# Gather, running sum and projection on one core: groups of four scheduled tiles against hand-ordered single tiles with smaller stores

The chip is one Trainium2, the kernel uses one of its cores, and the metric is the device time in microseconds (us) of one execution.

The names used below: PE is the engine of matmuls (TensorE), DVE the vector engine, ACT the scalar engine, POOL the GpSimd engine, which issues the gathers here, and SP issues loads and stores. The granted clock is the mean share of PE's full clock that the chip allowed.

## The reference, cut to what matters

```python
B, S, N, D = (16, 4096, 2048, 512)
gathered = x[b_idx, indices, :]          # x fp32 [B,S,D], indices int64 [B,N], sorted
cs = np.cumsum(gathered, axis=1)         # running sum along the N gathered rows
return np.matmul(cs, w)                  # w fp32 [D,D], result fp32 [B,N,D]
```

There are 16 x 2048 = 32,768 rows, or 256 tiles of 128 rows. 67 MB are read and 67 MB are written.

## The kernel before

A gather of one tile is an indirect DMA issued by POOL. It converts fp32 to fp16 on the way (the page of the kernel before has 68.42 MB read from HBM, and 33.57 MB moved by the gathers' queue). PE multiplies the tile by a triangular matrix, which gives the sums within the tile, transposed (`pa`). DVE adds the last column of the tile before and writes `csT`. PE multiplies `csT` by `w` (`pb`), ACT copies `pb` to `ob`, and SP stores `ob`. A group of R tiles is interleaved so that each partition holds R neighbouring output rows, which makes runs of R x 2 KB in the store.

```python
    R = 4; Q = P // R; AHEAD = 10                      # groups of four tiles; ten groups ahead
    gp  = tile_pool(name="gp", bufs=R * (AHEAD + 2))   # 48 gather buffers of 128 x 512 fp16
    csp = tile_pool(name="csp", bufs=4);  outp = tile_pool(name="outp", bufs=5)
    psA = tile_pool(name="psA", bufs=3, space=PSUM); psB = tile_pool(name="psB", bufs=5, space=PSUM)
    ... # indices: two loads of 128 rows, w: one load on ACT's queue
    for k in range(KI):                                # indices to one per partition
        nc.vector.tensor_copy(out=idxf[:, k, :], in_=idx64[:, k, :].bitcast(U32)[:, 0::2])
        nc.tensor.transpose(out=idx_ps[:], in_=idxf[:, k, :], identity=ident[:])
        nc.vector.tensor_copy(out=idxg[:, k, :], in_=idx_ps[:])
    ...
    for g in range(AHEAD):
        gather(g)                                      # four indirect DMAs
    for g in range(G + 1):
        if g + AHEAD < G:
            gather(g + AHEAD)
        for r in range(R):
            if g < G:
                cumsum_tile(g, r)                      # 4 matmuls pa, DVE add -> csT
            if g > 0:
                project_tile(g - 1, r)                 # 4 matmuls pb, ACT copy; r==3: store 1 MB
```

The order of instructions on each engine is chosen by a scheduler.

Of the kernel before, what the change touches and what calls it, by code (L numbers as in the profile page):

```python
# [1 line left out]

# [5 lines left out]

P = 128
FP32 = mybir.dt.float32  # L10
FP16 = mybir.dt.float16
U32 = mybir.dt.uint32
I64 = mybir.dt.int64


@with_exitstack
def kernel(
    ctx: ExitStack,
    tc: tile.TileContext,
    x: bass.AP,  # L20
    indices: bass.AP,
    w: bass.AP,
    out: bass.AP,
):
    nc = tc.nc

    B, S, D = x.shape
    N = indices.shape[1]
    R = 4
    Q = P // R  # L30
    DC = D // P
    NT = N // P
    T = B * NT
    G = T // R
    GB = NT // R
    AHEAD = 10
    assert D == 512 and N % (R * P) == 0 and T % P == 0

    x_flat = x.rearrange("b s d -> (b s) d")

    const = ctx.enter_context(tc.tile_pool(name="const", bufs=1))
    gp = ctx.enter_context(tc.tile_pool(name="gp", bufs=R * (AHEAD + 2)))
    csp = ctx.enter_context(tc.tile_pool(name="csp", bufs=4))
    outp = ctx.enter_context(tc.tile_pool(name="outp", bufs=5))
    psA = ctx.enter_context(tc.tile_pool(name="psA", bufs=3, space=bass.MemoryType.PSUM))
    psB = ctx.enter_context(tc.tile_pool(name="psB", bufs=5, space=bass.MemoryType.PSUM))


    KI = T // P
    idx_rows = indices.rearrange("b (t p) -> (b t) p", p=P)  # L50
    idx64 = const.tile([P, KI, P], I64)
    for k in range(KI):
        nc.sync.dma_start(out=idx64[:, k, :], in_=idx_rows[k * P : (k + 1) * P, :])  # L53
    w32 = const.tile([P, DC, D], FP32)
    nc.scalar.dma_start(out=w32[:], in_=w.rearrange("(c p) d -> p c d", p=P))

    ident = const.tile([P, P], FP32)
    make_identity(nc, ident[:])

    ut = const.tile([P, R, Q], FP16)  # L60
    nc.gpsimd.memset(ut[:], 1.0)  # L61
    nc.gpsimd.affine_select(  # L62
        out=ut[:],
        in_=ut[:],
        compare_op=mybir.AluOpType.is_ge,
        fill=0.0,
        base=0,
        pattern=[[1, R], [R, Q]],
        channel_multiplier=-1,
    )  # L70

    idxf = const.tile([P, KI, P], FP32)
    idxg = const.tile([P, KI, P], U32)
    for k in range(KI):
        nc.vector.tensor_copy(out=idxf[:, k, :], in_=idx64[:, k, :].bitcast(U32)[:, 0::2])  # L75
        idx_ps = psB.tile([P, P], FP32, name="idx_ps", tag="pb")
        nc.tensor.transpose(out=idx_ps[:], in_=idxf[:, k, :], identity=ident[:])  # L77
        nc.vector.tensor_copy(out=idxg[:, k, :], in_=idx_ps[:])  # L78

    w16 = const.tile([P, DC, D], FP16)  # L80
    nc.scalar.copy(out=w16[:], in_=w32[:])  # L81

    gs = {}
    cst = {}

    def gather(g):
        for r in range(R):
            t = g * R + r
            g16 = gp.tile([P, D], FP16, name="g16")
            nc.gpsimd.indirect_dma_start(  # L90
                out=g16[:],
                out_offset=None,
                in_=x_flat,
                in_offset=bass.IndirectOffsetOnAxis(ap=idxg[:, t // P, t % P : t % P + 1], axis=0),
                element_offset=(t // NT) * S * D,
            )
            gs[t] = g16

    def cumsum_tile(g, r):
        if r == 0:  # L100
            cst[g] = csp.tile([P, DC, R, P], FP16, name="csT")
        csT = cst[g]
        g16 = gs.pop(g * R + r)
        pa = psA.tile([P, DC, R, Q], FP32, name="pa")
        for c in range(DC):
            nc.tensor.matmul(  # L106
                out=pa[:, c],
                lhsT=g16[:, c * P : (c + 1) * P],
                rhs=ut[:],
                start=(c == 0),  # L110
                stop=(c == DC - 1),
            )
        dst = csT[:, :, :, r * Q : (r + 1) * Q]
        if g % GB == 0 and r == 0:
            nc.vector.tensor_copy(out=dst, in_=pa[:])  # L115
            return
        if r == 0:
            last = cst[g - 1][:, :, R - 1, P - 1 : P]
        else:
            last = csT[:, :, R - 1, r * Q - 1 : r * Q]  # L120
        nc.vector.tensor_tensor(  # L121
            out=dst,
            in0=pa[:],
            in1=last.unsqueeze(2).broadcast_to([P, DC, R, Q]),
            op=mybir.AluOpType.add,
        )

    obs = {}

    def project_tile(g, r):  # L130
        if r == 0:
            obs[g] = outp.tile([P, R, D], FP32, name="ob")
        csT = cst[g]
        pb = psB.tile([P, D], FP32, name="pb")
        for c in range(DC):
            nc.tensor.matmul(  # L136
                out=pb[:],
                lhsT=csT[:, c, r, :],
                rhs=w16[:, c, :],
                start=(c == 0),  # L140
                stop=(c == DC - 1),
            )
        nc.scalar.copy(out=obs[g][:, r, :], in_=pb[:])  # L143
        if r == R - 1:
            b, h = divmod(g, GB)
            dst = out[b, h * R * P : (h + 1) * R * P, :].rearrange("(p j) d -> p j d", j=R)
            nc.sync.dma_start(out=dst, in_=obs.pop(g)[:])

    for g in range(AHEAD):
        gather(g)  # L150
    for g in range(G + 1):
        if g + AHEAD < G:
            gather(g + AHEAD)
        for r in range(R):
            if g < G:
                cumsum_tile(g, r)
            if g > 0:
                project_tile(g - 1, r)
        cst.pop(g - 2, None)


# [1 line left out]
_INS = ['x', 'indices', 'w']  # L163
_OUTS = [((16, 2048, 512), 'float32')]


# [23 lines left out]
```

## Time and profile before

| | span of the profile | granted clock | timed |
|---|---|---|---|
| before, the profile given for the prediction | 364.5 us | 0.983 | 366.29 us |
| before, the timed runs | – | – | 448.89 us (447.04 to 449.05) |

The profile and the timed runs are 22.5% apart. In the slices below, the span is cut into 40 equal slices, and each digit is the busy share of one slice in tenths (9 is 90% or more).

### The profile page before, as it was taken

Reading aid. Unit: us, or ns where it says so; the run is one execution under the profiler, and the core shown is the slowest. Engines: PE = TensorE matmul, PEld = TensorE weight load, DVE = VectorE, ACT = ScalarE, POOL = GpSimd, SP = SyncE. Lnnn points to the kernel's source line nnn. Section 1 sums busy time; section 2 is a strip of 40 time slices with the busy share of each in tenths; the row PEclk is TensorE's granted clock in tenths of the full one; section 3 lists DMA queues with packets and bytes.
Section 4 is the critical chain, followed back from the end, with each engine's and each line's share of the span. In section 5 each row is a group of like instructions: output and inputs, shape, how many; then the busy total and the mean of one; then the engine's idle time right before and its main releaser. Section 6 shows DMA issues by size and latency. Waiting matters only on the chain.

```text
span 364.5 us, 5566 instructions
## 1 busy us (share of the span) xinstructions
PE 298.8 (82%) x2050; PEld 155.0 (43%) x2050; DVE 178.1 (49%) x260; ACT 153.2 (42%) x258; POOL 241.4 (66%) x264
## 2 busy tenths in 40 slices
PE   1497896978979796997959889888979889599893
PEld 0243453534435443543525444444435445254441
DVE  1444563645546463554636456555536536256450
ACT  3043453544435353443525444444425525245343
POOL 2777777776767776676757777777756757677600
PEclk9999999999999999999999999999989989989998
DMA  4799999999999999999999999999999999999995
GB/s 144 101 170 248 312 277 298 318 311 268 303 304 283 292 320 310 253 308 299 298 295 278 290 291 322 301 295 305 321 308 248 311 312 247 301 220 304 310 317 237
DMA packets 46924, 102.36 MB, mean 281 GB/s; under 512 B 5168, under 2 KB 38192, under 8 KB 38704
## 3 DMA queue, kind: packets, MB, share of 16 engines
q0 software_dynamic: 36864, 33.57, 59.5%
q1 hardware_dynamic: 9504, 67.38, 45.7%
q10 hardware_dynamic: 528, 1.05, 0.8%
q8 instruction: 16, 0.26, 0.3%
q14 instruction: 12, 0.10, 0.1%
HBM read 68.42 MB, written 67.11 MB: 372 GB/s over the span
## 4 chain that ended last, share of the span: by engine, by line
DMA 50%; PE 30%; POOL 12%; issue 6%; POOLq 0%; ACT 0%; DVE 0%; SPq 0%
DMA g<-in_x_dram,idxg 48%; PE pb L136 23%; POOL g L90 12%; PE pa L106 7%; DMA idx<-in_indices_dram 1%; POOLq L185 0%; ACT ob L143 0%; SPq L53 0%; DVE idxf L75 0%; DVE idxg L78 0%; POOLq L90 0%
## 5 line engine op out<-in xcount | busy, mean ns | idle before, releaser
L90 POOL DMA_INDIRECT g<-in_x_dram,idxg x256 | 240.3, 939 | 104.5 <-issue 39.0
L136 PE MATMUL pb<-w,csT 128*128 128x512 f16 x1024 | 267.2, 385 | 0.0
L121 DVE TENSOR_TENSOR csT<-pa,csT 128x512 f16<-128x512 f32 x240 | 166.0, 692 | 156.5 <-PE pa L106 156.1
L143 ACT COPY ob<-pb 128x512 f32<-128x512 f32 x256 | 150.1, 586 | 201.1 <-PE pb L136 200.3
L106 PE MATMUL pa<-ut,g 128*128 128x128 f16 x1024 | 102.3, 224 | 53.6 <-DMA g<-in_x_dram,idxg 53.1
L106 PEld LDWEIGHTS <-g 128*128 128x128 f16 x1024 | 74.2, 99 | 132.5 <-DMA g<-in_x_dram,idxg 90.5
L136 PEld LDWEIGHTS <-csT 128*128 128x128 f16 x1024 | 91.0, 99 | 64.2 <-issue 4.3
L115 DVE CAST csT<-pa 128x512 f16<-128x512 f32 x16 | 11.1, 692 | 13.9 <-PE pa L106 13.9
L77 PE MATMUL idx_ps<-ident,idxf 128*128 128x128 f32 x2 | 0.9, 461 | 6.4 <-DVE idxf L75 6.4
L75 DVE CAST idxf<-idx 128x128 f32<-128x128 uint32 x2 | 0.5, 228 | 6.4 <-DMA idx<-in_indices_dram 6.4
L81 ACT CAST w<-w 128x2048 f16<-128x2048 f32 x1 | 1.9, 1899 | 3.8 <-DMA w<-in_w_dram 3.8
L77 PEld LDWEIGHTS idx_ps<-ident,idxf 128*128 128x128 f32 x2 | 0.4, 182 | 6.7 <-issue 3.9
L81 ACT ACT_TABLE_LOAD x1 | 1.3, 1283 | 1.3 <-PEq L174 1.3
L78 DVE CAST idxg<-idx_ps 128x128 uint32<-128x128 f32 x2 | 0.6, 288 | 0.4 <-PE idx_ps L77 0.4
masks.py:197 POOL MEMSET ident<- 128x128 f32 x1 | 0.2, 204 | 0.3 <-POOLq L174 0.3
masks.py:199 POOL TENSOR_SCALAR_AFFINE_SELECT ident<-ident 128x128 f32<-128x128 f32 x1 | 0.3, 283 | 0.0
L174 POOL MEMSET const-float32-0.0<- 128x1 f32 x1 | 0.1, 98 | 0.3 <-issue 0.3
L62 POOL TENSOR_SCALAR_AFFINE_SELECT ut<-ut 128x128 f16<-128x128 f16 x1 | 0.3, 303 | 0.0
L61 POOL MEMSET ut<- 128x128 f16 x1 | 0.2, 202 | 0.0
L174 POOL MEMSET const-uint8-127<- 128x1 uint8 x1 | 0.1, 119 | 0.0
L174 POOL MEMSET const-bfloat16-1.0<- 128x1 bf16 x1 | 0.1, 112 | 0.0
L174 POOL MEMSET const-float32-1.0<- 128x1 f32 x1 | 0.1, 104 | 0.0
## 6 DMA issues: line engine op xcount, KB each, us to landing
out_dram<-ob SPq DMA_DIRECT2D x64, 1024.0 KB, 7.3
g<-in_x_dram,idxg POOLq DMA_INDIRECT x256, 8.2
w<-in_w_dram ACTq DMA_DIRECT2D x1, 1024.0 KB, 5.6
idx<-in_indices_dram SPq DMA_DIRECT2D x2, 128.0 KB, 4.0
```

Of the source, the lines that this page charges most:

```text
L62: nc.gpsimd.affine_select(out=ut[:], in_=ut[:], compare_op=mybir.AluOpType.is_ge, fill=0.0, base=0, pattern=[[1, R], [R, Q]], channel_mult ...
L75: nc.vector.tensor_copy(out=idxf[:, k, :], in_=idx64[:, k, :].bitcast(U32)[:, 0::2])
L77: nc.tensor.transpose(out=idx_ps[:], in_=idxf[:, k, :], identity=ident[:])
L78: nc.vector.tensor_copy(out=idxg[:, k, :], in_=idx_ps[:])
L81: nc.scalar.copy(out=w16[:], in_=w32[:])
L90: nc.gpsimd.indirect_dma_start(out=g16[:], out_offset=None, in_=x_flat, in_offset=bass.IndirectOffsetOnAxis(ap=idxg[:, t // P, t % P : t % ...
L106: nc.tensor.matmul(out=pa[:, c], lhsT=g16[:, c * P : (c + 1) * P], rhs=ut[:], start=(c == 0), stop=(c == DC - 1),)
L115: nc.vector.tensor_copy(out=dst, in_=pa[:])
L121: nc.vector.tensor_tensor(out=dst, in0=pa[:], in1=last.unsqueeze(2).broadcast_to([P, DC, R, Q]), op=mybir.AluOpType.add,)
L136: nc.tensor.matmul(out=pb[:], lhsT=csT[:, c, r, :], rhs=w16[:, c, :], start=(c == 0), stop=(c == DC - 1),)
L143: nc.scalar.copy(out=obs[g][:, r, :], in_=pb[:])
L174: nc = _bacc.Bacc("TRN2", target_bir_lowering=False, num_devices=1)
```

## The change

The intent is a hand-ordered pipeline whose unit is one tile of 128 rows. Groups have two tiles instead of four, so stores have 256 rows with runs of 4 KB. The first two tiles take indices that are loaded one per partition, so the first gathers need not wait for the transposed indices. The look-ahead is 44 tiles (it was 40). Instructions stay in program order. The diff is cut: left out are the indices read as pairs of 32-bit words, the building of `ident` moved behind `ut`, and the code that only follows from these lines.

```diff
-    R = 4
+    R = 2
-    AHEAD = 10
+    FIRST = 2
+    AHEAD = 44
-    gp = ... bufs=R * (AHEAD + 2)
+    gp = ... bufs=AHEAD + 4
-    csp bufs=4, outp bufs=5
+    csp bufs=5, outp bufs=10
+    ctx.enter_context(tc.manual_schedule())
+    idx_first = const.tile([P, FIRST, 2], U32)
+        nc.sync.dma_start(out=idx_first[:], in_=indices[0, 0 : FIRST * P]... one per partition)
-    nc.scalar.dma_start(out=w32[:], ...)
+    nc.sync.dma_start(out=w32[:], ...)          # behind the index loads
...
+    for t in range(FIRST):
+        gather(t)                               # from idx_first
     for k in range(KI): cast, transpose, copy   # now in this order for each k
+    for t in range(FIRST, AHEAD):
+        gather(t)
+    LAG = R
+    for t in range(T + LAG):
+        if t + AHEAD < T:
+            gather(t + AHEAD)
+        if t < T:
+            cumsum_tile(t)
+        if t >= LAG:
+            project_tile(t - LAG)
```

More of the change, by code (lines that the diff above doesn't have):

```diff
@@ L12 @@
 U32 = mybir.dt.uint32
-I64 = mybir.dt.int64
 @with_exitstack
@@ L33 @@
     T = B * NT
-    G = T // R
-    GB = NT // R
-    AHEAD = 10
+    FIRST = 2
+    AHEAD = 44
     assert D == 512 and N % (R * P) == 0 and T % P == 0
@@ L41 @@
     const = ctx.enter_context(tc.tile_pool(name="const", bufs=1))
-    gp = ctx.enter_context(tc.tile_pool(name="gp", bufs=R * (AHEAD + 2)))
-    csp = ctx.enter_context(tc.tile_pool(name="csp", bufs=4))
-    outp = ctx.enter_context(tc.tile_pool(name="outp", bufs=5))
+    gp = ctx.enter_context(tc.tile_pool(name="gp", bufs=AHEAD + 4))
+    csp = ctx.enter_context(tc.tile_pool(name="csp", bufs=5))
+    outp = ctx.enter_context(tc.tile_pool(name="outp", bufs=10))
     psA = ctx.enter_context(tc.tile_pool(name="psA", bufs=3, space=bass.MemoryType.PSUM))
     psB = ctx.enter_context(tc.tile_pool(name="psB", bufs=5, space=bass.MemoryType.PSUM))
+    ctx.enter_context(tc.manual_schedule())
+    idx_first = const.tile([P, FIRST, 2], U32)
+    with nc.allow_non_contiguous_dma(reason="a few indices, one per partition"):
+        nc.sync.dma_start(
+            out=idx_first[:],
+            in_=indices[0, 0 : FIRST * P].bitcast(U32).rearrange("(t p w) -> p t w", p=P, w=2),
+        )
     KI = T // P
-    idx_rows = indices.rearrange("b (t p) -> (b t) p", p=P)
-    idx64 = const.tile([P, KI, P], I64)
+    idx_rows = indices.bitcast(U32).rearrange("b (t q) -> (b t) q", q=2 * P)
+    idx64 = const.tile([P, KI, 2 * P], U32)
     for k in range(KI):
@@ L54 @@
     w32 = const.tile([P, DC, D], FP32)
-    nc.scalar.dma_start(out=w32[:], in_=w.rearrange("(c p) d -> p c d", p=P))
-    ident = const.tile([P, P], FP32)
-    make_identity(nc, ident[:])
+    nc.sync.dma_start(out=w32[:], in_=w.rearrange("(c p) d -> p c d", p=P))
     ut = const.tile([P, R, Q], FP16)
@@ L70, with gather, cumsum_tile @@
     )
+    ident = const.tile([P, P], FP32)
+    make_identity(nc, ident[:])
     idxf = const.tile([P, KI, P], FP32)
     idxg = const.tile([P, KI, P], U32)
-    for k in range(KI):
-        nc.vector.tensor_copy(out=idxf[:, k, :], in_=idx64[:, k, :].bitcast(U32)[:, 0::2])
-        idx_ps = psB.tile([P, P], FP32, name="idx_ps", tag="pb")
-        nc.tensor.transpose(out=idx_ps[:], in_=idxf[:, k, :], identity=ident[:])
-        nc.vector.tensor_copy(out=idxg[:, k, :], in_=idx_ps[:])
-    w16 = const.tile([P, DC, D], FP16)
-    nc.scalar.copy(out=w16[:], in_=w32[:])
-    gs = {}
-    cst = {}
-    def gather(g):
-        for r in range(R):
-            t = g * R + r
-            g16 = gp.tile([P, D], FP16, name="g16")
-            nc.gpsimd.indirect_dma_start(
-                out=g16[:],
-                out_offset=None,
-                in_=x_flat,
-                in_offset=bass.IndirectOffsetOnAxis(ap=idxg[:, t // P, t % P : t % P + 1], axis=0),
-                element_offset=(t // NT) * S * D,
-            )
-            gs[t] = g16
-    def cumsum_tile(g, r):
+    w16 = const.tile([P, DC, D], FP16)
+    g16s, cst, obs = {}, {}, {}
+    def gather(t):
+        g16s[t] = gp.tile([P, D], FP16, name="g16")
+        ap = idx_first[:, t, 0:1] if t < FIRST else idxg[:, t // P, t % P : t % P + 1]
+        nc.gpsimd.indirect_dma_start(
+            out=g16s[t][:],
+            out_offset=None,
+            in_=x_flat,
+            in_offset=bass.IndirectOffsetOnAxis(ap=ap, axis=0),
+            element_offset=(t // NT) * S * D,
+        )
+    def cumsum_tile(t):
+        g, r = divmod(t, R)
         if r == 0:
@@ L102, in cumsum_tile @@
         csT = cst[g]
-        g16 = gs.pop(g * R + r)
+        g16 = g16s.pop(t)
         pa = psA.tile([P, DC, R, Q], FP32, name="pa")
@@ L113, in cumsum_tile @@
         dst = csT[:, :, :, r * Q : (r + 1) * Q]
-        if g % GB == 0 and r == 0:
+        if t % NT == 0:
             nc.vector.tensor_copy(out=dst, in_=pa[:])
@@ L126, in cumsum_tile, with project_tile @@
         )
-    obs = {}
-    def project_tile(g, r):
+    def project_tile(t):
+        g, r = divmod(t, R)
         if r == 0:
@@ L144, in project_tile @@
         if r == R - 1:
-            b, h = divmod(g, GB)
+            b, h = divmod(g, NT // R)
             dst = out[b, h * R * P : (h + 1) * R * P, :].rearrange("(p j) d -> p j d", j=R)
             nc.sync.dma_start(out=dst, in_=obs.pop(g)[:])
-    for g in range(AHEAD):
-        gather(g)
-    for g in range(G + 1):
-        if g + AHEAD < G:
-            gather(g + AHEAD)
-        for r in range(R):
-            if g < G:
-                cumsum_tile(g, r)
-            if g > 0:
-                project_tile(g - 1, r)
-        cst.pop(g - 2, None)
+    for t in range(FIRST):
+        gather(t)
+    for k in range(KI):
+        nc.vector.tensor_copy(out=idxf[:, k, :], in_=idx64[:, k, 0::2])
+        idx_ps = psB.tile([P, P], FP32, name="idx_ps", tag="pb")
+        nc.tensor.transpose(out=idx_ps[:], in_=idxf[:, k, :], identity=ident[:])
+        nc.vector.tensor_copy(out=idxg[:, k, :], in_=idx_ps[:])
+    for t in range(FIRST, AHEAD):
+        gather(t)
+    nc.scalar.copy(out=w16[:], in_=w32[:])
+    LAG = R
[6 more added lines that the diff above has]
+            project_tile(t - LAG)
 _INS = ['x', 'indices', 'w']
```

## The prediction

> **What bounds the kernel now.** I read the page in this order: engine shares and slices, DMA queues, the chain, then the waits of the gathers, then start and end in order of time. First the shares and slices.
>
> ```profile
> PE 298.8 (82%) x2050; PEld 155.0 (43%) x2050; DVE 178.1 (49%) x260; ACT 153.2 (42%) x258; POOL 241.4 (66%) x264
> ...
> PEclk9999999999999999999999999999989989989998
> DMA  4799999999999999999999999999999999999995
> GB/s 144 101 170 248 312 277 298 318 311 268 303 304 283 292 320 310 253 308 299 298 295 278 290 291 322 301 295 305 321 308 248 311 312 247 301 220 304 310 317 237
> ```
>
> No compute engine is full, the clock is granted nearly throughout, and the DMA row is at 9 from the third slice to the last but one. Only the first two slices and the last leave DMA time unused, and GB/s reaches its level of about 300 only in the fifth slice, near 36 us. The queues say what fills it:
>
> ```profile
> q0 software_dynamic: 36864, 33.57, 59.5%
> q1 hardware_dynamic: 9504, 67.38, 45.7%
> ```
>
> q0 is the gathers (256 tiles x 128 rows of 2 KB read, 1 KB written after conversion, plus 16 semaphore packets each), q1 the stores (8192 packets of 8 KB). 59.5% + 45.7% = 105% of 364.5 us: the 16 engines are oversubscribed, and the two queues overlap a little. Per tile and engine that is 0.595 x 364.5 / 256 = 0.85 us for gathers and 0.457 x 364.5 / 256 = 0.65 us for stores. Against them PE needs, in the late stretch where it doesn't wait, 1.09 us for a tile (four matmuls into pa and four into pb; a new tile starts at 343.49, 344.58, 345.67), and POOL can issue a gather every 1.24 us (0.94 busy plus 0.30 issue), 256 x 1.24 = 318 us. The real pace, 60 us to 340 us, is 210 gathers in 280 us = 1.33 us. So DMA sets the middle, POOL's issue rate lies 7% under it, PE 18% under it.
>
> The chain of waits and the waits on the gathers agree:
>
> ```profile
> DMA 50%; PE 30%; POOL 12%; issue 6%; POOLq 0%; ACT 0%; DVE 0%; SPq 0%
> ```
>
> ```profile
> PEld L106 <- DMA g<-in_x_dram,idxg: 90.5, 84, 3.5
> PE pa L106 <- DMA g<-in_x_dram,idxg: 53.1, 59, 3.2
> POOL g L90 <- issue: 39.0, 128, 0.3
> POOL g L90 <- PE pa L106: 26.3, 49, 3.2
> POOL g L90 <- DMA g<-in_x_dram,idxg: 23.6, 48, 1.9
> ```
>
> PE waits for landings. POOL waits too, although 48 gather buffers lie there: the build shows each gather waiting for one of eight gather semaphores in rotation, so only eight gathers are in flight whatever the look-ahead. With 8.2 us from issue to landing (largest 12.1), eight in flight give 8.2 / 8 = 1.03 us a tile, but at the slow landings over 1.24 x 8 = 9.9 us they hold POOL. The changed kernel has the same eight, so 44 tiles ahead in place of 40 changes nothing.
>
> The start and the end, in order of time:
>
> ```profile
> 6.58 0.23 DVE L75 CAST idxf<-idx 128x128 f32<-128x128 uint32 x1 [2.75 <-DMA idx<-in_indices_dram]
> 6.72 0.28 DVE L78 CAST idxg<-idx_ps 128x128 uint32<-128x128 f32 x1
> ...
> 7.29 1.09 POOL L90 DMA_INDIRECT g<-in_x_dram,idxg  x1 [5.55 <-DVE idxg L78]
> ...
> 19.63 0.59 ACT L143 COPY ob<-pb 128x512 f32<-128x512 f32 x1 [11.32 <-PE pb L136]
> ```
>
> The first gather starts at 7.29, since the scheduler put both casts of the indices ahead of the first copy back, and the second load came late, beside the weights. The first output copy comes at 19.63, the first store at 24.09, after six tiles of pa (the build's order: 24 matmuls of pa, then 8 of pb). At the end the last gather lands near 354.0, twenty pb matmuls follow (4.58 us), the last copy ends at 359.5 and the last 1 MB store at 364.
>
> One thing stays unexplained: the profiled run took 366.29 us, the timed ones 448.89, 82.6 us or 22.5% more. Nothing in the page tells whether this is slower memory, slower clock, or a fixed cost. I carry both a scaled and an unscaled reading.
>
> [...] The trace has both queues active on the same engines and slower landings (8.2 us median) than the 3.4 us minimum[...]. [...] packets of 1024, 2048 and 8192 B of plain loads took 46, 84 and 309 ns (packet records, medians), a line of about 8 to 9 ns plus 0.0366 ns/B. [...] The trace has three such drops in the middle, of 3.4 us each, too few to matter.
>
> **The change, part by part.** Conversion in the gather, matmul counts (1024 + 1024), copies (256) and bytes stay; the steady order on PE, four of pa and four of pb in turn, stays.
>
> *Start.* The two first tiles take indices loaded one per partition. The old first index load let DVE start at 3.60; a smaller one, first on SP, should do so by 3.3 to 3.6. So the first gather starts near 3.5 instead of 7.29: 3.8 us. POOL then has 2 x 1.24 = 2.5 us of issue, until 6.0, by which the first 128 rows of indices (now cast, transposed, copied without waiting for the second load) are there, about 5.0 to 5.5. No hole. PE's first projection comes after three tiles instead of six, bounded by the weights (landing about 7 to 8, cast 1.9 us, so 10). The first store should come at 12 to 14 us in place of 24.09. This matters since before the stores begin the engines are partly idle. By the DMA share of stretches, the old kernel had done 8 x 0.46 + 12 x 0.72 + 16 x 1.00 = 28.3 us of DMA work by 36 us; the full rate after is 1.11. New: about 3.7 by 4.5 us, then 9.5 us at 0.80/1.24 = 0.64 with gathers alone, 9.8 in all by 14 us; the remaining 18.5 at 1.11 need 16.7 us: 30.7 instead of 36. Gain 5.3 us.
>
> *End.* Three tiles of pb are left after the last landing instead of five: 2 x 0.86 = 1.7 us. The last store is half as large: 0.5 MB at the loaded level is about 1.2 to 1.5 us less. Gain 3 us.
>
> *Stores.* 16,384 packets of 4 KB for 8192 of 8 KB. By the line above a 4 KB packet takes about 158 ns unloaded; in the loaded kernel 8 KB took 321 against 309, so I take 158 x 1.04 = 164, twice that is 328 for 321: 7 to 8 ns x 512 packets of 8 KB per engine = 4 us. The 64 more completion packets per engine add 64 x 20 ns = 1.3 us. Sum 5.4 us of engine time, at rate 1.11 4.9 us on the path. Loss 5 us, an estimate, the weakest term.
>
> *Look-ahead, buffers, DVE.* Output buffers stay 5 MB; stores wait for nobody but ACT now. DVE writes runs of 64 instead of 32 elements; it is busy half the time. Nothing.
>
> Sum: -5.3 - 3 + 5 = -3.3 us, in the profile 364.5 to 361. On the timed 448.89 that is 445.6 if the gap is a fixed cost, 444.8 if it is a factor.
>
> **Rivals.** (1) Smaller store packets help. [...] Gathers land more evenly, POOL's 50 us of holds on landings shrink, and pace goes from 1.33 to POOL's 1.24 us. For it: landings swing between 3.4 and 12.1 us. Against it: the engines are busy throughout[...]. At its full size 256 x 0.09 = 23 us less, 338 in the profile, about 425 timed. (2) The bytes decide, or in the timed runs a lower clock on PE (1.09 us of 1.33 is near enough that 0.65 of the clock would give the timed 1.7 us a tile): then only start and end count, 5 to 8 us, 440 to 444. (3) 4 KB runs cost more than the line says in the slower timed state, say 5% of the store's 165 us, 8 us more: 450 to 454. Halved lag could also expose DVE (0.69 us add) between pa and pb; the order keeps one projection and one pa group between, 1.2 us, so I give it little.
>
> **Range and chances.** The working gives 445; rival 1 in part, and that hand order is usually kept because it helped, draw me to 443. Range 430 to 451: below, half of rival 1 with the ends; above, rival 3. The border of faster is 439.9, which needs ends at full worth and free 4 KB packets, or some of rival 1: 0.30. Slower needs over 457.9: 0.07.
>
> **What would show it.** Right: first gather at 3 to 4 us, first store at 12 to 14, second slice of the DMA row at 9, q0 as before, q1's share up by one to two points, a 4 KB packet near 164 ns, landing to end about 7 us instead of 10, span 358 to 364. Rival 1 right: POOL's holds on landings well under 50 us, q0 + q1 over the span above 108%, pace below 1.30 us. Wrong altogether: the timed ratio departing from the profiled one by more than 2%, which would mean that what makes timed runs slow reacts to the size of stores or to the order, or a new wait of PE on csT.

Passages that no trace or run of this case shows are cut from it. No term of its sum is among them: start -5.3, end -3, stores +5, together -3.3 us, so 445.6 or 444.8 on the timed 448.89. Cut are a remark on the weight load's move to SP, which carries no term, the reason given for rival 1 (how an engine serves the two queues) and half of the argument against it, which were not shown; rival 1 stands as a guess. What stands of packets is from the packet records of the profile of 364.5 us: medians of 46 ns for 1024 B, 84 for 2048 B and 309 for 8192 B, and means of 20.3 and 17.2 ns for the 4 B completion packets of the gathers' and the stores' queues, called 20 ns. The three drops are of PE's granted clock: 0.50 for 3.4 us each, from 270.3, 294.2 and 318.1 us on. Rival 2's 0.65 of the clock is an estimate from 1.09 and 1.7 us; in the first of these drops four `pb` matmuls took 1.91 us, just before it 1.03.

## The result, and the profile after

The changed kernel took 443.44 us (442.82 to 443.97, 4 runs), and the kernel before took 448.31 us (447.04 to 449.05, 4 runs). The ratio is 0.9894, with a 95% interval of 0.9864 to 0.9924: within 2%. The predicted 443 us was met. Ratios here are the mean time of one kernel's fast runs over that of the other's of the same rounds, so not quite the ratio of the medians quoted.

The changed kernel's profile does not look like the profile that the prediction was worked from. These are the slices (PE, POOL, DMA) and the two busy queues of the changed kernel, from the page:

```profile
PE   2530030487777876877787777778776777899996
POOL 6777774366666665566666666666656666500000
DMA  8998887499999999999999999999999999975665
...
q0 software_dynamic: 36864, 33.57, 54.8%
q1 hardware_dynamic: 19520, 68.43, 40.2%
```

PE does little from the third to the seventh slice (22 to 77 us) while POOL issues gathers at full pace, until 72 us. At the end POOL has nothing left for five slices, and PE works at 9. The same rows of the unchanged kernel, run again on a chip where it takes about 449 us (e1_before):

```profile
PE   1614010097888697877868778695975897999994
POOL 3777777166665656556656665665655665300000
DMA  4788988299999999999999999999999999965656
```

It has the same hole. So the kernel before, in its timed state, loses some 60 us at the start, and the profile of 364.5 us is of a state without it. The chips of that profile and of the original timed runs are not on record. The hole in order of time, first DVE of e1_before (start, duration, instruction, and in brackets how long it was idle and what the profile names as the end of the wait):

```profile
17.91 0.69 DVE L121 TENSOR_TENSOR csT<-pa,csT 128x512 f16<-128x512 f32 x1 [0.52 <-DVE csT L121]
23.21 0.69 DVE L121 TENSOR_TENSOR csT<-pa,csT 128x512 f16<-128x512 f32 x1 [4.61 <-PE pa L106]
34.47 0.69 DVE L121 TENSOR_TENSOR csT<-pa,csT 128x512 f16<-128x512 f32 x1 [10.56 <-remote]
54.76 0.69 DVE L121 TENSOR_TENSOR csT<-pa,csT 128x512 f16<-128x512 f32 x1 [19.60 <-remote]
77.16 0.69 DVE L121 TENSOR_TENSOR csT<-pa,csT 128x512 f16<-128x512 f32 x1 [21.71 <-remote]
88.37 2.28 DVE L121 TENSOR_TENSOR csT<-pa,csT 128x512 f16<-128x512 f32 x3 [10.52 <-remote]
```

Then PE and DVE of the changed kernel:

```profile
23.27 0.63 PE L103 MATMUL pa<-ut,g 128*128 128x128 f16 x4
23.70 1.91 PE L132 MATMUL pb<-w,csT 128*128 128x512 f16 x4
25.40 0.63 PE L103 MATMUL pa<-ut,g 128*128 128x128 f16 x4
55.24 1.89 PE L132 MATMUL pb<-w,csT 128*128 128x512 f16 x4 [29.21 <-DVE csT L118]
```

```profile
32.79 0.69 DVE L118 TENSOR_TENSOR csT<-pa,csT 128x512 f16<-128x512 f32 x1 [11.26 <-issue]
54.49 0.69 DVE L118 TENSOR_TENSOR csT<-pa,csT 128x512 f16<-128x512 f32 x1 [21.01 <-remote]
76.89 0.69 DVE L118 TENSOR_TENSOR csT<-pa,csT 128x512 f16<-128x512 f32 x1 [21.71 <-remote]
```

The `pa` matmuls that start at 23.27 and at 25.40 are those of the eighth and the ninth tile, counted in program order, and are over by 26.1 us. The DVE adds that need them, the eighth and the ninth, start at 54.49 and 76.89: 31 and 51 us after PE was done. PE waits 29 us for the first of the two. DVE to PE is prompt (add ends 55.18, matmul starts 55.24); it is PE's completion that reaches DVE late. The profile names "remote" or "issue" where it finds no record of what released the wait. PE's completion updates in this stretch of the trace stand at 20.82, 25.06, 54.47, 66.37 and 76.87 us, some having no record, and from 20 us on DVE's and ACT's starts, taken in turn, follow each other at 4 to 12 us. A low clock of PE is not the cause: PE stands nearly idle in this stretch (4.45 us busy from 20 to 36 us and 4.45 from 36 to 60, at a granted clock of 0.50), and the pace after it is 1.50 us a tile in e5 and e7 too, where the granted clock of that part was 1.00 (shown below). The stretch ends when POOL first has to wait, with its 48 buffers filled: the gather at 77.13 is the 57th and needs the buffer of the ninth tile, whose add starts at 76.89. POOL of the changed kernel at that point:

```profile
71.47 0.94 POOL L87 DMA_INDIRECT g<-in_x_dram,idxg  x1 [0.30 <-issue]
77.13 0.94 POOL L87 DMA_INDIRECT g<-in_x_dram,idxg  x1 [4.73 <-remote]
82.80 0.94 POOL L87 DMA_INDIRECT g<-in_x_dram,idxg  x1 [4.74 <-remote]
```

From there both kernels go at 40 tiles in 60 us, 1.50 us a tile, until POOL is done, and PE then works off the backlog at 1.09 us a tile. The difference of the two spans, 447.7 - 442.2 = 5.5 us, lies at the two ends. The last gather starts at 385.6 in e1_before and at 383.5 in the changed kernel (2.1 us). From there to the end it is 62.1 and 58.7 us (3.4 us). By the prediction's measure, from the last `pa` to the end, it is 10.5 and 7.5 us.

### The profile page after: what moved, and what is told of

Its sections match the earlier page's. It is cut to its first block, busy times and chain, and to the rows that moved or that the text cites. A ratio compares the mean times of both kernels' runs of the same rounds, so it can differ in the third digit from the quotient of the medians.

```text
span 442.2 us, 5755 instructions
## 1 busy us (share of the span) xinstructions
PE 299.4 (68%) x2050; PEld 161.7 (37%) x2050; DVE 177.4 (40%) x260; ACT 153.0 (35%) x258; POOL 241.4 (55%) x264
## 4 chain that ended last, share of the span: by engine, by line
PE 69%; another core or an unknown queue 12%; issue 12%; DVE 3%; DMA 2%; ACT 2%; DVEq 0%
PE pb L132 52%; PE pa L103 17%; DVE csT L118 3%; ACT ob L139 2%; DMA g<-in_x_dram,idx_first 1%; DMA idx_first<-in_indices_dram 0%; DVE csT L112 0%; DVEq L118 0%
## 5 line engine op out<-in xcount | busy, mean ns | idle before, releaser
L132 PE MATMUL pb<-w,csT 128*128 128x512 f16 x1024 | 271.8, 389 | 130.5 <-DVE csT L118 72.9
L132 PEld LDWEIGHTS <-csT 128*128 128x128 f16 x1024 | 89.3, 100 | 204.0 <-DVE csT L118 76.2
L103 PEld LDWEIGHTS <-g 128*128 128x128 f16 x1024 | 80.7, 100 | 67.0 <-issue 5.5
L87 POOL DMA_INDIRECT g<-in_x_dram,idx_first x2 | 2.0, 1014 | 1.4 <-DMA idx_first<-in_indices_dram 1.0
```

What stands on the lines that cost most here:

```text
L87: nc.gpsimd.indirect_dma_start(out=g16s[t][:], out_offset=None, in_=x_flat, in_offset=bass.IndirectOffsetOnAxis(ap=ap, axis=0), element_of ...
L103: nc.tensor.matmul(out=pa[:, c], lhsT=g16[:, c * P : (c + 1) * P], rhs=ut[:], start=(c == 0), stop=(c == DC - 1),)
L132: nc.tensor.matmul(out=pb[:], lhsT=csT[:, c, r, :], rhs=w16[:, c, :], start=(c == 0), stop=(c == DC - 1),)
```

## The experiments

All were built from the changed kernel unless they say otherwise, and all were correct unless they say otherwise. A hold is a stretch in which DVE and ACT stand still although PE's work for them is done. Below, "a chip with holds" is one where the kernel before takes about 448 us, and "a chip without" is one where it takes about 361 us. The runs went to four chips: e1 to e4 to one with holds, e5 to e8 to another with holds, e9 and e10 to one without, e12 and e13 to another without. No chip was visited twice, so the chip is not told apart from whatever else differed between the batches; "chip" below stands for both.

### e1_before: the kernel before again (no edit)

> The unchanged kernel before, once more, to get a trace of it in the state in which it is timed. Stall theory (drawn from the trace of the changed kernel, where PE's results reach DVE and ACT 5 to 22 us late between 16 and 82 us, while POOL issues gathers without a pause): this run takes about 448 us, its trace shows the same holds of DVE and ACT between 15 and 90 us, and the profile of 366 us that I predicted from is another state of the same kernel. Rival, the DMA-bound picture of the prediction: a span of 448 us with packets about 22% longer and no such gap at the start, or again 366 us.

448.39 us (447.2 to 449.73); ratio to the kernel before 0.9994 (0.9935 to 1.0053). The holds are in the trace, as shown above. What the stall theory expected came: the holds belong to the timed state of the kernel before, and the profile behind the prediction is of another kind.

### e2_ahead12: less look-ahead

```diff
-    AHEAD = 44
+    AHEAD = 12
```

> The changed kernel with 12 tiles of look-ahead (16 gather buffers) instead of 44 (48 buffers). Stall theory: the holds end when POOL first has to wait for a buffer, so they end after some 16 tiles instead of 58, near 30 us instead of 82, and the time falls by 40 to 60 us, to 385 to 405 us. Rival, DMA-bound: eight gathers are in flight anyway, so the look-ahead is worth nothing: 441 to 446 us.

412.22 us (411.61 to 412.42); ratio 0.9191 (0.9142 to 0.924). That is less than I had expected (385 to 405), but clear. POOL meets its first missing buffer after the gather at 29.25 us, and the holds end there:

```profile
29.25 0.94 POOL L87 DMA_INDIRECT g<-in_x_dram,idxg  x1 [0.30 <-issue]
32.42 0.94 POOL L87 DMA_INDIRECT g<-in_x_dram,idxg  x1 [2.23 <-remote]
35.28 0.94 POOL L87 DMA_INDIRECT g<-in_x_dram,idxg  x1 [1.92 <-remote]
```

The expected end of the holds, near 30 us, was right; the pace after it, still 1.50 us, is why the gain is smaller. The prediction's statement that look-ahead changes nothing is refuted on this kind of chip.

### e3_r4: stores of 8 KB runs in the changed kernel

```diff
-    R = 2          # outp bufs=10
+    R = 4          # outp bufs=5
```

> The changed kernel with groups of four tiles: stores of 512 rows with 8 KB runs, lag of four tiles, as before; order, first indices and look-ahead as changed. The prediction's terms: stores of 4 KB cost about 5 us, the shorter lag gains about 3 us at the end and 2 at the start, so this run is within 1 us of 443.4 in either direction. Stall theory: the size of stores matters only after the stall, 440 to 447 us. If it goes back to 448 us, stores and lag carry the whole gain.

443.01 us (441.66 to 444.66); ratio 0.9882 (0.9822 to 0.9942). So with 8 KB runs and four tiles of lag the gain over the kernel before is the same. On a chip with holds, store size and lag together are worth nothing that can be seen. Whether each is worth nothing, or they cancel as the prediction's terms would (5 us against 3 and 2), this run can't tell. In its trace the last `pa` to the end takes 10.4 us instead of 7.5, while the last gather starts at 379.1 instead of 383.5.

### e4_nofirst: without the straight-loaded first indices

```diff
-        ap = idx_first[:, t, 0:1] if t < FIRST else idxg[:, t // P, t % P : t % P + 1]
+        ap = idxg[:, t // P, t % P : t % P + 1]      # FIRST = 0, idx_first and its load removed
```

> The changed kernel without the straight-loaded first indices: its first gather waits for the transposed indices, at about 4.6 us instead of 2.9. The prediction's start term: most of the gain at the start comes from the order of casts and copies and not from these loads, so 1.3 to 2 us slower than changed, 444.5 to 446 us. Stall theory: POOL reaches its first wait for a buffer 1.7 us later, also 1 to 2 us. If the time doesn't move, the early start is worth nothing.

445.46 us (443.72 to 446.92); ratio 0.9936 (0.9875 to 0.9997). Its first gather starts at 4.42 us instead of 2.94. Against e3_r4 on the same chip it is 2.4 us slower, and 2.0 us slower than the changed kernel's 443.44, whose chip is not on record. The intervals overlap, so it fits the expected 1.3 to 2 us and doesn't prove it.

### e5_ahead6: still less look-ahead

```diff
-    AHEAD = 44
+    AHEAD = 6
```

> The changed kernel with 6 tiles of look-ahead (10 buffers), fewer than the eight gathers that may be in flight. Stall theory: POOL has to wait for a buffer still sooner, the holds at the start end near 22 to 26 us, and the pace after stays at the 1.50 us a tile of the run with 12: 398 to 408 us. Rival (latency): with six or fewer gathers in flight the landings no longer cover the loop, the pace gets worse than 1.50 us, and the run is slower than the 412 us of 12 tiles.

405.47 us (405.17 to 405.71); ratio 0.9048 (0.9005 to 0.9091), the fastest correct version on the chips with holds. The pace did not suffer: 40 tiles in 60 us as before (DVE's and ACT's counts in this stretch of 60 us; after the engines' busy times stand the granted clock, the DMA share and GB/s):

```profile
120.00:180.00 60.00, 45.12 (x322) 24.52 (x319) 26.78 (x39) 22.88 (x40) 37.29 (x40) 1.00 1.06 263
```

An estimate from the traces: a tile of look-ahead that is filled during the holds costs POOL's 1.24 us, takes one tile of the 1.50 us part away, and is worked off at the end at 1.09 us, so 1.24 - 1.50 + 1.09 = 0.83 us. For 44 to 6 that is 38 x 0.83 = 32 us; measured 443.44 - 405.47 = 38 us, not in one batch.

### e6_pause: a pause on POOL after each gather

```diff
+        nc.gpsimd.memset(rest[:], 0.0)     # 128 x 128 fp32 scratch, after each gather
```

> The changed kernel, 44 tiles ahead, with a small memset of a scratch tile on POOL after each gather (0.2 us of work by the one in the start of the page, and POOL's wait for itself). [...] Theory A (PE's updates get through only in the pauses of POOL's gathers): the holds at the start vanish or shrink much, and the time falls below 425 us although POOL has more to do; POOL's own pace becomes about 1.5 us. Theory B (what holds the updates is the number of gathers in flight or the traffic as a whole, not POOL's instruction stream): holds stay, 443 us or more.

444.81 us (443.26 to 445.28); ratio 0.992 (0.9869 to 0.9972). Holds stay, so theory A gets no support, but the test was weak. The memset took POOL 0.23 us, but the gather after it had less issue time, so the period went only from 1.24 to 1.34 us instead of the expected 1.5 (the next gather starts at 24.49). From one gather's end to the next one's start it is 0.39 us instead of 0.30, with the memset in it, so POOL stood idle for less time than before:

```profile
22.77 0.23 POOL L95 MEMSET rest<- 128x128 f32 x1
23.16 0.95 POOL L88 DMA_INDIRECT g<-in_x_dram,idxg  x1 [0.17 <-issue]
```

### e8_pause_a12: pause and 12 tiles

Both edits of e2 and e6.

> The same memset after each gather, with 12 tiles of look-ahead. Theory A: no holds at the start, the pace is POOL's own, about 1.5 us: 395 to 410 us. Theory B: 412 us as with 12 tiles alone, or slower.

411.66 us (411.37 to 413.89); ratio 0.9204 (0.9153 to 0.9254): as with 12 tiles alone. The range expected by theory A reached to 410, so this adds little to e6, but agrees with it.

### e7_lag4: 12 tiles ahead, projections four tiles behind

```diff
-    LAG = R        # csp bufs=5
+    LAG = 2 * R    # csp bufs=7, and AHEAD = 12
```

> 12 tiles of look-ahead, and projections four tiles behind the cumulated sums instead of two (7 instead of 5 csT buffers). In the steady part PE works 4 x 1.09 us and waits 1.6 us out of 6.0 for DVE, whose inputs were announced late. If that wait for csT is the bound of the steady part, twice the lag hides it and the pace falls from 1.50 to 1.25 to 1.40 us: 350 to 390 us. Rival: PE waits for the two PSUM pools (3 and 5 buffers) just as long, since DVE and ACT are told late: 408 to 416 us.

407.57 us (406.55 to 408.46); ratio 0.91 (0.9053 to 0.9148). It lies outside both expectations, at the rival's edge. The steady pace is again 1.50 us:

```profile
120.00:180.00 60.00, 45.59 (x323) 24.67 (x322) 27.57 (x40) 22.65 (x41) 37.67 (x41) 1.00 1.09 266
```

So PE's wait for `csT` is not what sets the pace on the chips with holds. It moves elsewhere (here to waits before `pa`) while the pace stays. It is 4 us less than 12 tiles alone took in e2 (412.22), which ran on another chip; the steady pace being the same, they lie outside the steady part.

### e9_flight4: four gathers in flight

POOL copies one element of each partition of the tile gathered four before, so it waits for that tile's landing before it issues the next gather.

```diff
+        if t >= FLIGHT:                                   # FLIGHT = 4
+            nc.gpsimd.tensor_copy(out=seen[:], in_=g16s[t - FLIGHT][:, 0:1])
```

> The changed kernel, 44 tiles ahead and 48 buffers, but with at most four gathers in flight: before gather t POOL reads one element of tile t-4, so it waits for that landing. Theory B (PE's updates wait behind the backlog of gathers already handed to the DMA engines: eight of them at 1.3 us is the 11 us step between updates at the start): the steps at the start halve to about 5 us, PE gets twice as far in the stretch, and the time falls by 20 to 50 us, to 395 to 425 us. Theory C (the distance between POOL and PE, that is the number of filled buffers, is what counts): the holds last until POOL runs out of buffers as before, 440 us or more.

443.42 us (438.62 to 450.16), where the kernel before took 360.99 us (355.88 to 365.63): ratio 1.2283 (1.213 to 1.2435). This batch had gone to a chip without holds, so neither theory was tested; that question stays open. The profile is of its one slow run (450.16); its three fast runs took 438.62 to 443.78 us. What the run does show is what the number in flight is worth there. From issue to landing the profile says:

```profile
DMA to landing us min/median/max: 3.3/5.8/8.5
```

With half as many in flight a landing takes 5.8 us instead of the 9.1 of the changed kernel on such a chip (e13), so not half as long. 35 gathers instead of 46 start in 60 us. PE's `pa` waits 110.2 us for landings, where in e13 it is 35.3. The loop looks bound by latency there.

### e10_halfstore: 6 tiles ahead, every second group stored (wrong)

```diff
-        if r == R - 1:
+        if r == R - 1 and g % 2 == 0:
```

> 6 tiles of look-ahead, and only every second group is stored: the result is wrong on purpose. It asks what sets the 1.50 us a tile of the steady part. If the DMA engines do (gathers 0.94 + stores 0.67 us of packets a tile at a share of 1.07): without half of the stores the pace falls to (0.94 + 0.34) / 1.07 = 1.2, so to POOL's 1.24 us, and the time to 335 to 350 us. If the late updates of PE set it: 1.45 to 1.5 us still, 395 to 405 us.

332.96 us (332.68 to 334.26); ratio 0.9267 (0.9191 to 0.9343), result wrong as meant. It is a little below the expected 335 to 350. It ran on the same chip without holds as e9, so it answers for that kind of chip. With half of the stores gone the pace is POOL's own: the last gather starts at 320.2 us, and (320.2 - 5.6) / 253 = 1.24 us. So PE can keep a pace of 1.24 us, and it is the stores' DMA work, not PE, that makes the pace of about 1.32 us there. (Six tiles ahead with all stores were not run on such a chip; the 1.32 us is of kernels with more look-ahead.) For the 1.50 us of the chips with holds it was not answered.

### e12_before_a2: the kernel before, two groups ahead

```diff
-    AHEAD = 10
+    AHEAD = 2
```

> The kernel before with two groups of four tiles of look-ahead (16 gather buffers) instead of ten (48). On a chip where the kernel before takes about 448 us and shows the holds at the start: the look-ahead is the lever in it too, 412 to 420 us, within 2% of the changed kernel with 16 buffers (412.22), so most of what separates 448 from 405 is the look-ahead and not the change. On a chip where the kernel before takes about 361 us without holds: nothing, 358 to 364 us, since eight gathers are in flight with either.

360.99 us (358.27 to 363.07) beside 362.93 us (357.91 to 366.42); ratio 1.0021 (0.9887 to 1.0155), on a chip without holds. There, look-ahead beyond the gathers in flight is worth nothing, as the prediction had said. Whether it helps the kernel before on a chip with holds was not run; that it has the same holds and the same 48 buffers makes it likely and no more.

### e13_after: the changed kernel, unaltered

> The changed kernel, unaltered, beside the above. On a chip where the kernel before takes about 448 us: 442 to 445 us again. On a chip where it takes about 361 us: the prediction's own sum, made from a trace of that kind, start -5.3, end -3, small stores +5, so 3 us less than before, 356 to 361 us; rival 1 of the prediction (small packets let the gathers land evenly, pace 1.24 us) 338 to 348 us.

355.78 us (354.65 to 356.82) beside 362.93 us (357.91 to 366.42); ratio 0.9899 (0.9793 to 1.0005), on the same chip as e12. This is the run that the prediction had really been worked out for. The interval reaches past 1, so the gain isn't clear of noise here. The kernel before scatters: of its seven runs those at 357.9 to 358.7 us had granted clocks of 0.991 to 0.996, the slowest, 366.42, had 0.974, but one of 364.98 had 0.990, so the clock doesn't explain the scatter. The changed kernel had 0.993 to 0.998 in all four. The ratio uses only the fast ones; their means differ by 3.6 us.

## Why the prediction was right, point by point

**The total** came out for the right terms on the wrong kind of chip. The working was made from a trace of 364.5 us of a chip without holds; its sum of -3.3 us was then carried over to the timed 448.89 us. On both kinds of chip the measured gain is about 1% (0.9894 and 0.9899, the second not clear of noise). Luck had a part. The working itself gave 445; the 443 that was met leaned on a part of rival 1, that smaller stores help, which the runs don't show at work. And on a chip with holds the gain is made of other pieces than those added up: 2.1 us up to the last gather and 3.4 after it. On the chip of e13, for which the working fits, the fast runs differ by 3.6 us, near the -3.3, though its profile's span, 353.9, lies below the announced 358 to 364. That the 82.6 us between them were neither a factor nor a fixed cost, but a stall at the start plus a slower steady pace, the prediction left open, and did not foresee.

**DMA bounds the middle: right where there are no holds.** The page of e13_after, against the rows quoted in the prediction:

```profile
DMA  7999999999999999999999999999999999999995
...
q0 software_dynamic: 36864, 33.57, 59.4%
q1 hardware_dynamic: 19520, 68.43, 50.1%
```

The second slice is at 9, as announced, and q0's share is as before. q1's is up by 4.4 points (from 45.7%), more than the one to two announced; 0.8 points of that are the weight load (1.05 MB) that moved onto it from q10, and part of the rest is the shorter span. One of rival 1's signs came with that, q0 + q1 above 108% (109.5%); its other two did not (see small stores). e10 shows the bound by taking stores away.

With holds it is not so. These are waits of the changed kernel in the profile of the result (us in total, times, longest):

```profile
PE pb L132 <- DVE csT L118: 72.9, 14, 29.2
POOL g L87 <- PE pa L103: 61.0, 47, 1.5
PE pa L103 <- DMA g<-in_x_dram,idx_first: 3.5, 1, 3.5
POOL g L87 <- DMA g<-in_x_dram,idxg: 0.6, 2, 0.3
```

POOL waits 61.0 us for PE to free buffers and 0.6 us for landings, and PE waits for the landing of one gather only, the first. In the kernel of the prediction's profile it was 26.3 and 23.6 us for POOL and 53.1 us for PE.

**Start, -5.3 us: right in size, one step late.** From e13_after, in order of time:

```profile
2.94 1.09 POOL L87 DMA_INDIRECT g<-in_x_dram,idx_first  x1 [1.05 <-DMA idx_first<-in_indices_dram]
...
8.37 1.90 ACT L154 CAST w<-w 128x2048 f16<-128x2048 f32 x1 [6.28 <-DMA w<-in_w_dram]
...
15.78 12.76 SPq L143 DMA_DIRECT2D out_dram<-ob  x6
```

The first gather starts at 2.94 (said: 3.5), and POOL has no hole after it. The first store comes at 15.78, later than the 12 to 14 that were said. That the first gathers share the engines with the weights may be why (the first `pa` starts at 9.02); no run tested it. Counted as in the prediction, by DMA share, the kernel before (first fence) and the changed one (second) had done by 36 us:

```profile
0.00:8.00 8.00, 0.92 (x2) 0.36 (x2) 0.95 (x4) 2.87 (x2) 1.80 (x9) 1.00 0.46 164
8.00:20.00 12.00, 5.76 (x30) 3.04 (x31) 4.15 (x6) 0.68 (x2) 8.95 (x11) 1.00 0.72 94
20.00:36.00 16.00, 13.70 (x92) 6.66 (x89) 7.61 (x11) 6.66 (x12) 12.08 (x13) 1.00 1.00 220
```

```profile
0.00:8.00 8.00, 0.92 (x2) 0.36 (x2) 0.95 (x4) 1.28 (x1) 5.05 (x12) 1.00 0.69 183
8.00:20.00 12.00, 10.61 (x63) 5.55 (x64) 5.79 (x9) 5.31 (x7) 9.19 (x10) 1.00 0.95 154
20.00:36.00 16.00, 12.06 (x82) 5.61 (x81) 6.95 (x11) 5.89 (x11) 11.81 (x14) 1.00 1.12 278
```

8 x 0.69 + 12 x 0.95 + 16 x 1.12 = 34.8 against 28.3 us of work, 6.5 more, which at 1.13 are 5.8 us. Against e12, the kernel before with less look-ahead on e13's own chip, it is 5.9 more, or 5.2 us. Said were 5.3. On the chips with holds most of this is lost: POOL is up to 4.35 us earlier at the start, but the last gather starts only 2.1 us earlier.

**End, -3 us: right on both.** Without holds, the kernel before and then the changed one:

```profile
354.27 4.58 PE L136 MATMUL pb<-w,csT 128*128 128x512 f16 x20
...
346.43 0.40 PE L103 MATMUL pa<-ut,g 128*128 128x128 f16 x4 [0.58 <-DMA g<-in_x_dram,idxg]
346.67 2.85 PE L132 MATMUL pb<-w,csT 128*128 128x512 f16 x12
```

Twelve matmuls are left instead of twenty (2.85 against 4.58 us). From the last landing to the end it is 353.9 - 346.4 = 7.5 us instead of 364.5 - 354.0 = 10.5, and 10.5 in e12 too. With holds it is 7.5 instead of 10.5 as well.

**Small stores, +5 us: the packet's cost was right, the net is not shown.** Packets of 4 KB took 166.7 ns in the mean (said 164), and all stores of the kernel 170.7 us of an engine instead of 164.5. But the gathers' packets took 100.4 ns instead of 103.3, 205.6 us instead of 211.5, which the prediction had not counted. If that is an effect of the smaller stores, the net term is near zero instead of +5. The profile before, however, is of a slow run whose chip is not on record. Against e12, a fast run of the kernel before on e13's chip, though with less look-ahead, the stores took 7.6 us more, the gathers 5.1 us less, and all packets of an engine together 3.6 us more (388.9 against 385.3), where 5.4 were said. Nor do the times decide it. With 5.2 to 5.8 us at the start, 3.0 at the end and nothing for the stores the sum is -8.2 to -8.8; with the predicted 5 it is about -3 to -4. The two spans, 364.5 and 353.9, differ by 10.6, but the first is of a slow run; the fast runs differ by 3.6, and those of the kernel before alone spread over 5 us (357.9 to 362.9). No run without holds changed the store size alone.

Rival 1 did not come in its main part: POOL's waits on landings and releases did not shrink (26.3 + 23.6 + 9.9 = 59.8 us before, 31.1 + 20.9 + 8.9 = 60.9 us in e13, for pa, gathers and pb as the profile books them), and 180 gathers against 179 started between 60 and 300 us. The prediction's "50 us of holds on landings" was misread: 26.3 of them are waits for PE, and only 23.6 for landings. Another reading of it doesn't hold either: the packets of 8192 B at 309 ns, called plain loads, are 19 packets of an instruction queue. It doesn't carry the result. What brings the three clock drops in the middle is not shown.

**Look-ahead, "changes nothing": right without holds (e12), wrong with them (e2, e5).** The step that failed is the argument that eight gathers are in flight whatever the look-ahead, and so buffers beyond eight are idle. Eight in flight the trace of 364.5 us does show: its gathers take eight semaphores in turn, and wherever all landings are on record (124 pairs) the gather eight later started 0.26 us or more after the landing. But the buffers beyond eight are not idle while PE is held up: POOL fills them (56 gathers started by 71.47 us in the changed kernel), PE loses that time, and only the backlog's faster end pays some of it back. It did not hurt this prediction because the change left the buffers at 48.

**What stays open.** Why PE's completions reach DVE and ACT late on some chips. It is not the kernel alone, since the same kernel has it in some batches and not in others; it goes with the chip or with whatever else differed between the batches (four chips: two with, two without, each visited once). POOL's lack of pauses got no support (e6), in a weak test. The backlog of gathers in flight could be it, as eight at the 1.3 us a tile of the prediction's profile would be 10.4 us (an estimate), near some of the steps seen (10.5 to 11.3 us); e9 was meant to test it and landed on the wrong kind of chip. On the chips with holds the traces also hold fewer of PE's completion records than there should be (390 in the changed kernel, 359 in e2, against 516 in e13) and of the landings of gathers (1539 of 4096, where e13 has all). Longer gather packets are no mark of holds: their mean is 115.8 ns in the changed kernel, but 117.2 in e10 on a chip without. Whether the recording itself takes part cannot be told, since every timed run here was recorded with its span and clock. And what sets the 1.50 us a tile there: neither lag (e7), nor POOL's period (e6, e8), nor look-ahead moved it. The DMA share is 1.05 to 1.09 in that part, but PE of the changed kernel waits for no landing there. What its trace shows is a DVE add that starts late once in four tiles, that is in 6.0 us: a `pa` is over at 242.6, its add starts at 244.46, and PE stands idle for 1.50 us before it goes on at 245.21. So PE's late updates may set this pace too; that is not shown.

## What to carry to other kernels

When the profile and the timed runs differ by a fifth, get a profile of the timed state before trusting any view of the other; compare pages slice by slice, and look first for a stretch where one engine races and the rest stand still. A small change at the start and end of a pipeline can be priced by counting the DMA work done by a given time, where the DMA engines set the pace; here that was checked on one chip. And buffers ahead of the consumer are not free insurance: give as many as are needed to cover what is in flight, here 6 instead of 44 tiles, which took 8.6% off the changed kernel's time on one kind of chip (405.47 against 443.44 us); on the other kind, 8 to 11 tiles in place of 40 cost the kernel before nothing, and 6 tiles ran there only with half of the stores.
